# TensorE's order in the attention of a hybrid block: an even spread, and an order from a model of three engines' clocks

## The chip, the cores and the metric

One core of one Trainium2 chip runs the whole program. The metric is the device time of one execution in microseconds. The kernel before took 2173.42 us (median of 3 runs, 2172.76 to 2175.5). Engines are named as the profile names them: PE is TensorE (PEld its weight loads), DVE is VectorE, ACT is ScalarE, POOL is GpSimd, SP is SyncE, whose queue issues most DMAs.

## What is computed

One block of a hybrid model in float32, for 1024 tokens of width 1024: a norm, a projection to nine streams, a gated linear recurrence with 8 heads, a stick-breaking attention with 16 heads of width 64, output projections and a gated feed-forward. The change lies in the attention:

```python
def stick_breaking(q, k, v):
    scale = 1.0 / float(np.sqrt(SB_DH))
    outs = []
    for blk in range(s_len // SB_BLOCK):          # 8 rows of 128 queries
        q0 = blk * SB_BLOCK
        end = q0 + SB_BLOCK
        z = jnp.einsum('bhqd,bhkd->bhqk', q[:, :, q0:end], k[:, :, :end]) * scale
        mask = kpos[None, :] < qpos[:, None]
        log_keep = jnp.where(mask, jax.nn.log_sigmoid(-z), 0.0)
        log_w = jax.nn.log_sigmoid(z) + lax.cumsum(log_keep, axis=3, reverse=True) - log_keep
        a = jnp.where(mask, jnp.exp(log_w), 0.0)
        outs.append(jnp.einsum('bhqk,bhkd->bhqd', a, v[:, :, :end]))
```

q and k are normalised per head before it.

## The kernel before

The program has a recurrence stage, then the attention, then the output projections and the feed-forward. The attention works on 8 pairs of heads (`p`), each with two heads (`j`), and each head on 4 groups (`g`) of two query rows (`i`) of 128. Four kinds of work of a pair stand on TensorE:

- A **score** (`chunk`, L739 and L740) multiplies a query row with 1 to 4 blocks of 128 keys into a PSUM bank `pz`, of which there are two. ScalarE then makes two sigmoids of it (L749: `kp`, what is kept, and `a`), VectorE runs a scan backwards over `kp` (L752 or L755) and multiplies `a` by it (L757). Four tiles `a` exist. A row of more than four blocks is cut into two chunks (`KEY_CHUNKS`), so a pair has 24 scores.
- A **turn** (L782) transposes the up to four blocks of `a` that belong to two key blocks and two query rows into a bank `pt` (two banks). ScalarE copies the high half `th` (L784), VectorE subtracts for the low half `tl` (L785), three tiles of each.
- An **apply** (L798 and L799) multiplies `th` and `tl` with the values into the bank `po`, of which there is one. The last apply of a group is followed by a copy on ScalarE (L803), an addition on VectorE (L804) and a store. `reads` puts an apply two turns behind its own turn; a pair has 20 of each.
- **Fill** is other work that needs no attention result: the projections of the next pair's keys and queries, and of values or gates, in steps of three matmuls with 512 columns (0.65 units) or with 256 (0.33 units). Between its steps stand the norms of the next pair: the key sums (L275, L276), the query sums (L668, whose operands GpSimd makes in L646 and L647), the roots on VectorE (L679 to L691), and the normalising of the keys (L701 to L708), whose results SP's DMAs copy to the other head. `at_fill` gives the units of fill after which each of these comes.

TensorE's order is that of the calls in the program; nothing reorders it. The other engines' orders are made from the program by a scheduler, with the split of a turn at high priority. `at_pair` returns one list: it spreads the scores of a group evenly over the reads of the group before it, with constants. `weave` then spreads the fill over that list in proportion to costs written beside each step (`1.954 * max(nb, 2) * 0.054` for a score, 0.406 for a turn, 0.583 for an apply), after 2.854 units of fill ahead of the first score.

Of the kernel before, what the change touches and what calls it, by code (L numbers as in the profile page):

```python
# [35 lines left out]
def hybrid_block(ctx, tc, x, norm1_gain, w_in, lb_logits, hg_out_norm, sb_q_norm, sb_k_norm,  # L36
# [3 lines left out]
    x, out = x[0], out[0]  # L40
# [14 lines left out]
    def pbank(tag, bufs=2):  # L55
        return pp.tile([P, HS], F32, tag=tag, bufs=bufs, name=tag)
# [293 lines left out]
    def hg_q(h):  # L350
        return proj_t(in_block(h * P), copy_half(hd[h], "q"))
# [309 lines left out]
    def at_qn(p, half):  # L661
        def go():
            d = ad[p]
            sq = d.pop(("sq", half))
            pq = pbank("pz")
            for i in range(4):
                for j in range(3):
                    nc.tensor.matmul(pq[:, 2 * i:2 * i + 2], sq[:, j, i * P:(i + 1) * P], blk2, start=j == 0, stop=j == 2)  # L668
            nc.vector.tensor_copy(d["nv"][:, 16 + 8 * half:24 + 8 * half], pq[:, 0:8])
        return [(0.86, go)]  # L670
# [55 lines left out]
    def at_pair(p):  # L726
        d = ad[p]
        v, rq = d["v"], d["rq"]
        rows_of = {}

        def chunk(j, g, i, end, nb, first):
            def go():
                kk = d["kk"][j]
                qhi, qlo = d["qh"][j][i // 4], d["ql"][j][i // 4]
                qs = slice((i % 4) * P, (i % 4 + 1) * P)
                k0, w = (end - nb) * P, nb * P
                n = max(w, 256)
                ps = pbank("pz")
                nc.tensor.matmul(ps[:, :n], qhi[:, qs], kk[:, k0:k0 + n], start=True, stop=False)  # L739
                nc.tensor.matmul(ps[:, :n], qlo[:, qs], kk[:, k0:k0 + n], start=False, stop=True)  # L740
                if first:
                    d["kp"] = kps[0]
                    kps.append(kps.pop(0))
                at0 = (NT - 1 - i) * P + k0
                kp = d["kp"][:, at0:at0 + w + 1]
                a = at.tile([P, HS], F32, tag="a", bufs=4, name="a")
                col = 2 * i + j
                for n_, t in enumerate((kp, a)):
                    nc.scalar.activation(t[:, 0:w], ps[:, 0:w], AF.Sigmoid, scale=rq[:, n_, col:col + 1])  # L749
                rev = kp[:, 0:w][:, ::-1]  # L750
                if first:
                    nc.vector.tensor_tensor_scan(rev, rev, dsel[:, HS - w:][:, ::-1], initial=0.0,  # L752
                                                 op0=ALU.mult, op1=ALU.max)
# [3 lines left out]
                nc.vector.tensor_mul(a[:, 0:w], a[:, 0:w], kp[:, 1:w + 1])  # L757
# [12 lines left out]

        def turn(j, g, m):
            def go():
                tp = pbank("pt")
                th = at.tile([P, HS], F32R, tag="th", bufs=3, name="th")
                tl = at.tile([P, HS], F32R, tag="tl", bufs=3, name="tl")
                c0 = P if m == g else 0
                for s, (kb, i) in enumerate([(2 * m + 1, 2 * g), (2 * m + 1, 2 * g + 1),
                                             (2 * m, 2 * g), (2 * m, 2 * g + 1)]):
                    if m == g and s == 0:
                        continue  # L780
                    a, b = rows_of.pop((j, i, kb))
                    nc.tensor.transpose(tp[:, s * P:(s + 1) * P], a[:, b * P:(b + 1) * P], ident)  # L782
                with tc.high_priority():
                    nc.scalar.copy(th[:, c0:], tp[:, c0:])  # L784
                    nc.vector.tensor_sub(tl[:, c0:], tp[:, c0:], th[:, c0:].bitcast(F32))  # L785
                d["t", j, g, m] = th, tl
            return 0.406, go

        def apply(j, g, m):
            def go():  # L790
                if m == g:
                    d["po"] = pbank("po", 1)
                po = d["po"]
                th, tl = d.pop(("t", j, g, m))
                for u in (1, 0):
                    kb, c0 = 2 * m + 1 - u, P if m == g and u == 0 else 0
                    sl = slice(256 * u + c0, 256 * u + 256)
                    nc.tensor.matmul(po[:, c0:256], v[:, kb, j, :], th[:, sl], start=kb == 2 * g, stop=False)  # L798
                    nc.tensor.matmul(po[:, c0:256], v[:, kb, j, :], tl[:, sl], start=False,  # L799
                                     stop=m == 0 and u == 0)  # L800
# [18 lines left out]
        for n, jg in enumerate(groups):  # L819
            a = reads(*jg)  # L820
            b = scores(*groups[n + 1]) if n + 1 < len(groups) else []
            length = sum(c for c, _ in a)
            own += [(start + length * (i + 0.5) / len(a), 1, i, s) for i, s in enumerate(a)]
            own += [(max(0.5, start + length * 0.855 * (i + 0.4) / len(b) - 0.039), 0, i, s)
                    for i, s in enumerate(b)]
            start += length
        return [s for *_, s in sorted(own, key=lambda x: x[:3])]

    def at_fill(p, mid):
        k, q = at_k(p), at_q(p)  # L830
        m = [s for f in mid for s in f()]
        out, t = k[:14] + at_kn(p, 0) + k[14:], 0.0
        extra = [(3.9, at_kn(p, 1)), (8.49, at_qn(p, 0)), (13.7, at_qn(p, 1) + at_roots(p)), (17.6, at_norm(p))]
        for s in q + m:
            while extra and t >= extra[0][0]:
                out += extra.pop(0)[1]
            out.append(s)
            t += s[0]
        return out

    weave([], at_fill(0, [lambda: at_v(0)]))
    for p in range(NPAIR):
        own = at_pair(p)
# [275 lines left out]
    for f in range(2, NF):  # L1119
        n = [(f + 1, m) for m in (1, 2)] if f + 1 < NF else []  # L1120
# [223 lines left out]
```

## Time and profile before

| what | value |
|---|---|
| median of 3 runs | 2173.42 us |
| the profiled execution, its own time | 2172.1 us |
| its span (first to last instruction) | 2170.3 us |
| mean granted clock of TensorE | 0.986 |
| recurrence and first projections, up to the attention's fill | 0 to 533 us |
| fill ahead of pair 0 | 533 to 585 us |
| attention, first score to last apply | 585.4 to 1222.0 us |
| output projections and feed-forward | 1222 to 2170 us |

In the profile's rows a group of instructions has its line, its engine, its operation, the tile it writes and those that it reads, and its count; a number in square brackets is the idle time of the engine just before it, with what ended it. Rows of waits have the total, the number of waits and the longest. The length of the attention is the distance between starts of pairs, which repeat with small differences: an even pair has 64 wide steps of fill, an odd one 32 wide and 64 narrow, and the last pair 48 wide ones and no norms.

### The profile page before, as it was taken

The numbers are of one execution on the slowest core, as the hardware profiler recorded it, in microseconds if no ns is written. First come the engines' busy times: TensorE is split into PE (matmuls) and PEld (weight loads), VectorE is DVE, ScalarE is ACT, GpSimd is POOL, SyncE is SP. The second block draws the span as 40 slices with busy tenths as digits, with TensorE's granted clock in tenths as the row PEclk, the third lists the DMA queues.
The fourth block names the chain that finished last, engine by engine and source line by source line (L and its number), as shares of the span: only waits on it lengthen the run. The fifth ranks groups of instructions, "written<-read, shape, count | busy, mean of one in ns | idle before, by whom it ended". The sixth has DMA issues, their size and how long they took to land. (4 is left out here: it accounts for less than half of the span.)

```text
span 2170.3 us, 29182 instructions
## 1 busy us (share of the span) xinstructions
PE 2050.4 (94%) x10981; PEld 1734.7 (80%) x10981; DVE 1459.1 (67%) x2108; ACT 1040.9 (48%) x1791; POOL 735.1 (34%) x488
## 2 busy tenths in 40 slices
PE   7999999999899999998998989989799999999999
PEld 7889798988877877877877778767688888887787
DVE  6575848575387787787787698999733333337975
ACT  4453444443366565565565554536433333333443
POOL 4443434353221121131221042142655555545000
PEclk9999999999999999999999999999899999999999
DMA  4211111122322232222222535513222312255221
GB/s 153 80 49 59 59 59 59 42 71 84 95 77 72 77 80 70 76 76 74 76 75 76 182 114 199 182 29 110 83 64 78 102 60 81 68 175 204 88 95 51
DMA packets 190605, 195.59 MB, mean 90 GB/s; under 512 B 11960, under 2 KB 135280, under 8 KB 190464
## 3 DMA queue, kind: packets, MB, share of 16 engines
q1 hardware_dynamic: 189456, 192.02, 28.4%
q8 instruction: 86, 1.41, 0.3%
q10 hardware_dynamic: 1008, 1.70, 0.2%
q14 instruction: 55, 0.45, 0.1%
HBM read 138.77 MB, written 38.14 MB: 82 GB/s over the span
## 5 line engine op out<-in xcount | busy, mean ns | idle before, releaser
L121 POOL TENSOR_TENSOR wl<-wr,wh 128x1024 fp32r<-128x1024 f32 x72 | 183.2, 2548 | 596.6 <-ACT wh L120 456.2
L138 PE MATMUL pd<-hT,wh 128*128 128x512 f32 (+1 forms) x920 | 377.3, 410 | 0.0
L140 PE MATMUL pd<-hT,wl 128*128 128x512 f32 (+1 forms) x920 | 357.6, 389 | 0.0
L139 PE MATMUL pd<-hT,wh 128*128 128x512 f32 (+1 forms) x920 | 357.2, 388 | 0.1
L887 ACT CAST wh<-u 128x512 fp32r<-128x512 f32 (+1 forms) x280 | 183.9, 684 | 229.1 <-PE po L140 68.2
L888 DVE TENSOR_TENSOR wl<-u,wh 128x512 fp32r<-128x512 f32 (+1 forms) x196 | 171.7, 912 | 51.1 <-ACT wh L887 46.2
L139 PE MATMUL pd<-u,wh 128*128 128x512 f32 x496 | 194.2, 392 | 10.5 <-DVE u L888 10.5
L140 PEld LDWEIGHTS pd<-hT,wl 128*128 128x128 f32 x920 | 174.2, 189 | 36.9
L138 PE MATMUL pd<-u,wh 128*128 128x512 f32 x496 | 194.6, 392 | 1.3 <-ACT c L1192 0.7
L139 PEld LDWEIGHTS pd<-hT,wh 128*128 128x128 f32 x920 | 175.6, 191 | 20.4 <-DVE hT L188 0.4
L138 PEld LDWEIGHTS pd<-hT,wh 128*128 128x128 f32 x920 | 175.3, 191 | 20.5 <-ACT hT L187 0.2
L884 POOL TENSOR_TENSOR u<-u,u 128x1024 f32<-128x1024 f32 (+1 forms) x46 | 105.8, 2318 | 193.4 <-DVE u L995 52.5
L752 DVE TENSOR_TENSOR_SCAN kp<-kp,dsel 128x512 f32<-128x512 f32 (+3 forms) x128 | 136.5, 1066 | 33.6 <-ACT kp L749 32.9
L749 ACT ACTIVATE kp<-pz,rq 128x128 f32<-128x128 f32 (+2 forms) x192 | 112.6, 587 | 80.9 <-PE pz L740 80.4
L138 PE MATMUL pd<-wh,hT 128*128 128x256 f32 x512 | 151.0, 295 | 0.0
L139 PE MATMUL pd<-wl,hT 128*128 128x256 f32 x512 | 147.0, 287 | 0.0
L140 PE MATMUL pd<-wh,hT 128*128 128x256 f32 x512 | 147.0, 287 | 0.0
L140 PE MATMUL pd<-u,wh 128*128 128x512 f32 x352 | 137.5, 391 | 0.0
L782 PE MATMUL pt<-ident,a 128*128 128x128 f32 x576 | 94.2, 282 | 37.3 <-DVE a L757 25.2
L757 DVE TENSOR_TENSOR a<-a,kp 128x128 f32<-128x128 f32 (+2 forms) x192 | 116.9, 609 | 16.9 <-ACT a L749 0.6
L784 ACT CAST th<-pt 128x512 fp32r<-128x512 f32 (+1 forms) x160 | 86.5, 547 | 85.3 <-PE pt L782 84.6
L782 PEld LDWEIGHTS pt<-ident,a 128*128 128x128 f32 x576 | 68.1, 143 | 67.6 <-DVE a L757 26.1
(266 smaller groups left out, 5097.9 us busy)
## 6 DMA issues: line engine op xcount, KB each, us to landing
wr<-in_w_in SPq DMA_DIRECT2D x72, 512.0 KB
u<-in_w_ffn_in SPq DMA_DIRECT2D x24, 512.0 KB
wr<-in_w_ffn_in SPq DMA_DIRECT2D x20, 512.0 KB
u<-in_w_ffn_out SPq DMA_DIRECT2D x10, 1024.0 KB
d_act<-c SPq DMA_DIRECT2D x33, 256.0 KB
u<-d_act SPq DMA_DIRECT2D x8, 1024.0 KB
qh<-qh SPq DMA_DIRECT2D x48, 128.0 KB
ql<-ql SPq DMA_DIRECT2D x48, 128.0 KB
```

Of the source, the lines that this page charges most:

```text
L121: nc.gpsimd.tensor_sub(lo, raw, hi.bitcast(F32))
L138: nc.tensor.matmul(ps, lh, rh, start=start, stop=False, skip_group_check=adds)
L139: nc.tensor.matmul(ps, lh, rl, start=False, stop=False, skip_group_check=adds)
L140: nc.tensor.matmul(ps, ll, rh, start=False, stop=stop, skip_group_check=adds)
L749: nc.scalar.activation(t[:, 0:w], ps[:, 0:w], AF.Sigmoid, scale=rq[:, n_, col:col + 1])
L752: nc.vector.tensor_tensor_scan(rev, rev, dsel[:, HS - w:][:, ::-1], initial=0.0, op0=ALU.mult, op1=ALU.max)
L757: nc.vector.tensor_mul(a[:, 0:w], a[:, 0:w], kp[:, 1:w + 1])
L782: nc.tensor.transpose(tp[:, s * P:(s + 1) * P], a[:, b * P:(b + 1) * P], ident)
L784: nc.scalar.copy(th[:, c0:], tp[:, c0:])
L884: e.tensor_tensor(raw(to), raw(a), raw(b), op=op)
L887: nc.scalar.copy(hi, src)
L888: e.tensor_sub(lo, src, hi.bitcast(F32))
```

## The change

`at_pair` now returns two lists, the scores and the reads, each in its own order. A new function, `flow`, takes the place of `weave` for the pairs. It keeps a clock each for TensorE, ScalarE and VectorE (`now`, which goes on from pair to pair), adds a written duration to them for each step that it calls, and chooses the next step by them: the next turn or apply when the model has its operands and its bank ready at most 0.05 us ahead of TensorE's clock, else the next score when fewer than four tiles `a` are held and one of the two banks is free, else one step of fill, else it moves TensorE's clock. What is left of the fill follows when scores and reads are used up. There is no fill ahead of a pair's first score any more. `at_fill` puts the norms later: 10.4, 15.4 and 19.5 units in place of 8.49, 13.7 and 17.6. The steps themselves are unchanged, and so is the number of instructions on every engine.

```diff
@@ at_pair @@
-            return 1.954 * max(nb, 2) * 0.054, go
+            return go
...
-                    steps.append(chunk(j, g, i, end, nb, end == i + 1))
+                    steps.append(((j, i, end - nb, nb), chunk(j, g, i, end, nb, end == i + 1)))
...
-            return 0.406, go
+            needs = [(j, i, kb) for kb in (2 * m + 1, 2 * m) for i in (2 * g, 2 * g + 1) if kb <= i]
+            return "turn", (j, g, m), needs, go
...
-            return 0.583, go
+            return "apply", (j, g, m), [], go
...
-        own, start, at_time = [(0.0, 0, n, s) for n, s in enumerate(scores(*groups[0]))], 1.0, 1.0
...
-            own += [(start + length * (i + 0.5) / len(a), 1, i, s) for i, s in enumerate(a)]
-            own += [(max(0.5, start + length * 0.855 * (i + 0.4) / len(b) - 0.039), 0, i, s)
-                    for i, s in enumerate(b)]
-            start += length
-        return [s for *_, s in sorted(own, key=lambda x: x[:3])]
+        return [s for jg in groups for s in scores(*jg)], [s for jg in groups for s in reads(*jg)]
+    now = {"pe": 0.0, "act": 0.0, "dve": 0.0}
+    def on(e, ready, took):
+        now[e] = max(now[e], ready) + took
+        return now[e]
+    def flow(score, read, fill):
+        made, split_at, left = {}, {}, {}
+        pz, pt, po = [0.0, 0.0], [0.0, 0.0], [0.0]
+        while score or read:
+            ready = None
+            if read:
+                kind, at_, needs, go = read[0]
+                if kind == "turn":
+                    ready = max([made.get(b, 1e9) for b in needs] + [min(pt)])
+                else:
+                    ready = max([split_at[at_]] + (po if at_[2] == at_[1] else []))
+            if read and ready <= now["pe"] + 0.05:
+                read.pop(0)
+                go()
+                if kind == "turn":
+                    end = on("pe", 0.0, 0.109 * len(needs) + 0.1)
+                    w = 0.15 + 0.0012 * 90 * len(needs)
+                    end = on("dve", on("act", end, w), w + 0.08)
+                    split_at[at_] = end + 0.3
...
+                else:
+                    end = on("pe", 0.0, 0.48)
...
+            elif score and len(left) < 4 and min(pz) <= now["pe"] + 0.05:
+                c, go = score.pop(0)
+                go()
+                left[c] = c[3]
+                end = on("pe", 0.0, 0.114 * max(c[3], 2))
+                end = on("act", end, 2 * (0.26 + 0.109 * c[3]))
...
+                end = on("dve", end, 0.47 + 0.38 * c[3])
+                for b in range(c[2], c[2] + c[3]):
+                    made[c[0], c[1], b] = end + 0.4
+            elif fill:
+                c, go = fill.pop(0)
+                go()
+                t0 = now["pe"]
+                on("pe", 0.0, 1.05 * c)
+                on("act", t0, 0.3 * c)
+                on("dve", t0, 0.25 * c)
+            else:
...
+        for c, go in fill:
+            go()
...
-        extra = [(3.9, at_kn(p, 1)), (8.49, at_qn(p, 0)), (13.7, at_qn(p, 1) + at_roots(p)), (17.6, at_norm(p))]
+        extra = [(3.9, at_kn(p, 1)), (10.4, at_qn(p, 0)), (15.4, at_qn(p, 1) + at_roots(p)), (19.5, at_norm(p))]
...
-        weave(own, fill, lead=2.854)
+        flow(*at_pair(p), fill)
```

TensorE in pair 0, the first head's group 1, at its first turn. Before, a fill step, a three-block score and another fill step stand ahead of the three transposes (of `a`, into `pt`):

```order
L138 MATMUL pd<-hT_101,wh 128x512
L139 MATMUL pd<-hT_102,wh 128x512
L140 MATMUL pd<-hT_101,wl 128x512
L739 MATMUL pz<-kk,qh 128x384
L740 MATMUL pz<-kk,ql 128x384
L138 MATMUL pd<-hT_101,wh 128x512
L139 MATMUL pd<-hT_102,wh 128x512
L140 MATMUL pd<-hT_101,wl 128x512
L782 MATMUL pt<-ident,a 128x128 x3
```

Now the last of four fill steps and the apply of group 0 stand there, and two turns follow each other (an apply's lines are one higher in the changed kernel):

```order
L138 MATMUL pd<-hT_101,wh 128x512
L139 MATMUL pd<-hT_102,wh 128x512
L140 MATMUL pd<-hT_101,wl 128x512
L799 MATMUL po<-th,v 128x256
L800 MATMUL po<-tl,v 128x256
L799 MATMUL po<-th,v 128x128
L800 MATMUL po<-tl,v 128x128
L782 MATMUL pt<-ident,a 128x128 x7
```

Both group 1's turns and the scores ahead of them have moved together into clumps, with the fill steps between the clumps.

TensorE in the same head's group 2, from its second turn on. Before, each turn and score has a fill step behind it:

```order
L782 MATMUL pt<-ident,a 128x128 x4
L138 MATMUL pd<-hT_99,wh 128x512
L139 MATMUL pd<-hT_100,wh 128x512
L140 MATMUL pd<-hT_99,wl 128x512
L739 MATMUL pz<-kk,qh 128x384
L740 MATMUL pz<-kk,ql 128x384
```

Now two scores, the third turn and the group's first apply follow the second turn without fill, and one fill step stands ahead of the second apply:

```order
L739 MATMUL pz<-kk,qh 128x512
L740 MATMUL pz<-kk,ql 128x512
L739 MATMUL pz<-kk,qh 128x384
L740 MATMUL pz<-kk,ql 128x384
L782 MATMUL pt<-ident,a 128x128 x4
L799 MATMUL po<-th,v 128x256
L800 MATMUL po<-tl,v 128x256
L799 MATMUL po<-th,v 128x128
L800 MATMUL po<-tl,v 128x128
L138 MATMUL pd<-hT_99,wh 128x512
L139 MATMUL pd<-hT_100,wh 128x512
L140 MATMUL pd<-hT_99,wl 128x512
```

The fill has left the way from the second turn to its apply.

ScalarE at that place: the weight cast, the evacuation of the next pair's keys (`kr`, `sq`), a sigmoid, and then the copies `th` of the turns. Before:

```order
L120 CAST wh<-wr 128x1024
L618 ACTIVATE kr<-pd,cols 128x512
L620 ACTIVATE sq<-pd 128x512
L749 ACTIVATE kp_4506<-pz,rq 128x512
L784 CAST th<-pt 128x384
L784 CAST th<-pt 128x512
```

Now:

```order
L784 CAST th<-pt 128x384
L120 CAST wh<-wr 128x1024
L618 ACTIVATE kr<-pd,cols 128x512
L620 ACTIVATE sq<-pd 128x512
L749 ACTIVATE kp_4506<-pz,rq 128x512
L784 CAST th<-pt 128x512 x2
```

The first turn's copy has moved ahead of the key evacuation; the second turn's copy stands behind it and a sigmoid. At the end of each pair, on TensorE, 12 wide fill steps (26 narrow ones in an odd pair) now follow the last apply without anything between them, where one or two wide or narrow ones and then the 5 ahead of the next pair's first score stood.

More of the change, by code (lines that the diff above doesn't have):

```diff
@@ L817, in at_pair @@
         groups = [(j, g) for j in range(2) for g in range(4)]
-        own, start, at_time = [(0.0, 0, n, s) for n, s in enumerate(scores(*groups[0]))], 1.0, 1.0
[L819 to L822, printed above, removed]
-            own += [(start + length * (i + 0.5) / len(a), 1, i, s) for i, s in enumerate(a)]
-            own += [(max(0.5, start + length * 0.855 * (i + 0.4) / len(b) - 0.039), 0, i, s)
-                    for i, s in enumerate(b)]
-            start += length
@@ L827, in at_pair @@
-        return [s for *_, s in sorted(own, key=lambda x: x[:3])]
+        return [s for jg in groups for s in scores(*jg)], [s for jg in groups for s in reads(*jg)]
[4 more added lines that the diff above has]
+    def flow(score, read, fill):
+        score, read, fill = list(score), list(read), list(fill)
+        made, split_at, left = {}, {}, {}
[16 more added lines that the diff above has]
+                    split_at[at_] = end + 0.3
+                    pt.remove(min(pt))
+                    pt.append(end)
+                    for b in needs:
+                        c = next(c for c in left if c[0] == b[0] and c[1] == b[1] and c[2] <= b[2] < c[2] + c[3])
+                        left[c] -= 1
+                        if not left[c]:
+                            del left[c]
+                else:
+                    end = on("pe", 0.0, 0.48)
+                    if at_[2] == 0:
+                        end = on("act", end, 0.37)
+                        on("dve", end, 0.41)
+                        po[0] = end
+            elif score and len(left) < 4 and min(pz) <= now["pe"] + 0.05:
[4 more added lines that the diff above has]
+                end = on("act", end, 2 * (0.26 + 0.109 * c[3]))
+                pz.remove(min(pz))
+                pz.append(end)
+                end = on("dve", end, 0.47 + 0.38 * c[3])
[9 more added lines that the diff above has]
+            else:
+                now["pe"] = max(now["pe"], min([x for x in [ready, min(pz)] if x and x > now["pe"]], default=0.0)) + 0.01
+        for c, go in fill:
+            go()
+            t0 = now["pe"]
+            on("pe", 0.0, 1.05 * c)
+            on("act", t0, 0.3 * c)
+            on("dve", t0, 0.25 * c)
@@ L842, in hybrid_block @@
     for p in range(NPAIR):
-        own = at_pair(p)
         if p == NPAIR - 1:
```

## The prediction

> **What bounds the kernel now.** I read the page first for the length of the run and for the engine that fills it.
>
> ```profile
> span 2170.3 us, 29182 instructions
> PE 2050.4 (94%) x10981; PEld 1734.7 (80%) x10981; DVE 1459.1 (67%) x2108; ACT 1040.9 (48%) x1791; POOL 735.1 (34%) x488
> ```
>
> TensorE (PE) is said to be busy for 94% of 2170.3 us, so any gain must be idle time of TensorE. The edit touches only the attention, so next I cut the span by stage with the view of windows. The attention's first score stands at 585.4 and its last apply ends at 1222.0. The cuts inside are the starts of pairs: 667.23 (pair 1), 748.00 (pair 2), 830.33 (pair 3), 1157.64 (pair 7). A row has the stretch, its length, then busy time of PE, PEld, DVE, ACT and POOL, the granted clock, the DMA share and GB/s.
>
> ```profile
> 585.00:1220.00 635.00, 585.91 (x3549) 500.31 (x3548) 495.87 (x813) 396.36 (x767) 138.29 (x88) 0.98 0.28 75
> 667.23:748.00 80.77, 76.09 (x518) 68.50 (x516) 63.17 (x110) 50.94 (x100) 17.80 (x13) 0.98 0.25 64
> 748.00:820.00 72.00, 65.31 (x367) 53.53 (x366) 61.75 (x99) 47.15 (x92) 16.93 (x12) 0.98 0.31 82
> 748.00:830.33 82.33, 75.64 (x421) 62.34 (x420) 63.55 (x102) 50.32 (x96) 19.21 (x13) 0.98 0.32 87
> 1157.64:1222.00 64.36, 58.32 (x331) 48.03 (x330) 52.73 (x75) 42.14 (x83) 6.63 (x4) 1.00 0.17 53
> ```
>
> The reader is to see two things. TensorE idles 635.0 - 585.9 = 49.1 us in the attention, four tenths of the 119.9 us that it idles in the whole run. And inside pair 2 VectorE (DVE) is busy 61.75 of the first 72.00 us, but 63.55 - 61.75 = 1.80 of the last 10.33: while attention work lasts, VectorE runs at 86%. What TensorE waits for is in the view of waits, for this stage:
>
> ```profile
> PE pt L782 <- DVE a L757: 25.2, 27, 2.0
> PE pt L782 <- DVE tl L785: 11.4, 15, 1.5
> PE po L799 <- DVE tl L785: 5.0, 7, 1.0
> PE pz L668 <- POOL sq L647: 3.7, 3, 1.2
> PE pz L668 <- POOL sq L646: 2.3, 3, 0.8
> ```
>
> Turns wait for products of VectorE (25.2), turns wait for a free bank (11.4), applies wait for splits (5.0), and the query norm waits for GpSimd (6.0).
>
> Matmuls are pipelined, so a wait costs more than its idle time. I therefore rebuilt a pair from the distances between starts in stretches without waiting:
>
> ```profile
> 679.33 0.27 PE L798 MATMUL po<-th,v 128*128 128x256 f32 x1
> 679.73 0.44 PE L275 MATMUL pz<-sqh,blkr 128*128 128x512 f32 x1
> ...
> 681.29 0.27 PE L798 MATMUL po<-th,v 128*128 128x256 f32 x1
> ...
> 681.76 0.40 PE L138 MATMUL pd<-hT,wh 128*128 128x512 f32 x1
> ...
> 682.45 0.39 PE L739 MATMUL pz<-kk,qh 128*128 128x512 f32 x1
> ...
> 682.91 0.39 PE L138 MATMUL pd<-hT,wh 128*128 128x512 f32 x1
> ...
> 684.61 0.60 PE L782 MATMUL pt<-ident,a 128*128 128x128 f32 x4
> 684.97 0.48 PE L138 MATMUL pd<-hT,wh 128*128 128x512 f32 x1
> 685.28 0.39 PE L139 MATMUL pd<-hT,wh 128*128 128x512 f32 x1
> ...
> 685.75 0.33 PE L739 MATMUL pz<-kk,qh 128*128 128x384 f32 x1
> ...
> 686.10 0.39 PE L138 MATMUL pd<-hT,wh 128*128 128x512 f32 x1
> ...
> 742.29 0.28 PE L138 MATMUL pd<-wh,hT 128*128 128x256 f32 x1
> ...
> 742.65 0.28 PE L138 MATMUL pd<-wh,hT 128*128 128x256 f32 x1
> ```
>
> A wide fill step takes 682.45 - 681.76 = 0.69, a narrow one 0.36, a score of four blocks 0.46, of three 0.35 (so of two, and of one, which is padded to two, 0.23). A turn of four takes 684.97 - 684.61 = 0.36 and slows the matmul behind it from 0.23 to 0.31, so 0.44; a turn of three 0.33. An apply takes 0.47, the first of a group 0.40 (to 679.73); a key norm, two matmuls as wide as a fill step's, about 0.5. A pair has 24 scores (2 x (3 x 0.23 + 5 x 0.35 + 4 x 0.46) = 8.6), 20 turns (8 x 0.33 + 12 x 0.44 = 7.9), 20 applies (8 x 0.40 + 12 x 0.47 = 8.8) and two key norms (1.0): 26.3 us of its own; the narrow query matmuls, under 1 us, are left out. An even pair has 64 wide fill steps (44.2), an odd one 32 wide and 64 narrow (22.1 + 23.0), pair 7 in the old order 43 wide behind its first score (29.7) and no norm. Gapless this is 70.5, 71.4 and 55.0 us against 82.3, 80.8 and 64.4. **What TensorE loses is 11.8, 9.4 and 9.4 us a pair**, 4 x 11.8 + 3 x 9.4 + 9.4 = 85 us in all. That is the ceiling of this edit.
>
> **The change, part by part.** No instruction is added or removed; 192 scores, 160 turns, 160 applies and the fill steps stand in another order on TensorE, and the other engines' queues follow. Outside the attention only the fill ahead of pair 0 moves, by its norms.
>
> *Scores to turns.* In the order of before, group 1's first turn stands behind its last score (four blocks) by three wide steps, an apply and a score, 3 x 0.69 + 0.40 + 0.35 = 2.8 us, and waits there, in pair 1 for 1.13 us:
>
> ```profile
> 675.81 0.55 PE L782 MATMUL pt<-ident,a 128*128 128x128 f32 x3 [1.13 <-DVE a L757]
> ```
>
> In the new order there stand seven wide steps, a turn, two scores and an apply, 7 x 0.69 + 0.33 + 0.35 + 0.23 + 0.40 = 6.1 us. What VectorE has to do for a chunk, and the start of a pair, are these rows:
>
> ```profile
> L752 DVE TENSOR_TENSOR_SCAN kp<-kp,dsel 128x512 f32<-128x512 f32 x36 | 49.7, 1382 | 1.2 <-ACT kp L749 0.9
> L785 DVE TENSOR_TENSOR tl<-pt,th 128x512 fp32r<-128x512 f32 x72 | 49.2, 683 | 23.1 <-ACT th L784 22.8
> L752 DVE TENSOR_TENSOR_SCAN kp<-kp,dsel 128x384 f32<-128x384 f32 x36 | 40.0, 1111 | 5.9 <-ACT kp L749 5.8
> L757 DVE TENSOR_TENSOR a<-a,kp 128x512 f32<-128x512 f32 x48 | 37.4, 779 | 4.1 <-ACT a L749 0.6
> L757 DVE TENSOR_TENSOR a<-a,kp 128x384 f32<-128x384 f32 x60 | 34.4, 573 | 5.3 <-ACT th L784 0.5
> ```
>
> Four blocks are 1.38 + 0.78 = 2.16 us, three are 1.68. A four-block score with a three-block one queued ahead and a split makes some 4.5 us, plus its way through ScalarE: 6.1 covers it, 2.8 did not. So most of the 25.2 and 11.4 us should go.
>
> *Turns to applies.* The shortest way from a turn to its finished split, with both engines waiting for it, is this (822.28 to 823.53 + 0.69 = 1.94 us):
>
> ```profile
> 822.28 0.60 PE L782 MATMUL pt<-ident,a 128*128 128x128 f32 x4
> 822.91 0.59 ACT L784 CAST th<-pt 128x512 fp32r<-128x512 f32 x1 [2.34 <-PE pt L782]
> 823.53 0.69 DVE L785 TENSOR_TENSOR tl<-pt,th 128x512 fp32r<-128x512 f32 x1 [2.24 <-ACT th L784]
> ```
>
> Here the new order is not everywhere good. In group 2 the second turn is followed by two scores, a turn, an apply and one fill: 0.44 + 0.46 + 0.35 + 0.44 + 0.40 + 0.69 = 2.8 us to its apply, while ScalarE's queue has three operations about as long as the copy ahead of it, two of the key's evacuation and a sigmoid, some 2 us. 1.94 + 2 - 2.8 leaves 1.1; with VectorE late as well I take 1.7 us. In the second half of a pair the same place has even less cover (about 1 us), the last group's first turn finds a VectorE with three chunks, two splits and root steps to do (nothing to 1.5, I take 1), and the last applies have 1.75 us of cover against 1.94 (0.5). **Stalls left: 1.7 + 1 + 1 + 0.5 = 4.2 us a pair**; from below nothing, from above the 11.8 of now.
>
> *Fewer handovers.* Turns stand in 16 runs a pair in place of 20: 4 x 0.08 = 0.3 us.
>
> *Later query and key norms.* The first query norm moves from 8.49 to 10.4 units of fill; half 0 of the query then has 8 fill steps (5.5 us) and some 4 us of scores, turns and applies for GpSimd in place of 6 steps. The 6.0 us of waits are inside the 85 and are taken to go. The fill ahead of pair 0 has the same wait, in the view of waits from 533 to 586:
>
> ```profile
> PE pz L668 <- POOL sq L646: 2.1, 2, 1.7
> PE pz L668 <- POOL sq L647: 1.5, 2, 1.0
> ```
>
> Of these 3.6 us I take 2 to go: six more narrow steps, 2.2 us, stand ahead of the second query norm there. That is between nothing and 3.6.
>
> Key normalisation comes later on VectorE, behind the last four splits, and the next pair's first score needs its copies. 12 wide or 26 narrow fill steps (8.3 or 9.4 us) now stand after the last apply, and hide that.
>
> *What is late next: VectorE.* Those 12 steps have no attention work beside them. So pair 2 cannot be shorter than VectorE's work before them:
>
> ```profile
> 667.23 0.28 PE L739 MATMUL pz<-kk,qh 128*128 128x256 f32 x1
> ...
> 668.07 0.42 DVE L752 TENSOR_TENSOR_SCAN kp<-kp,dsel 128x128 f32<-128x128 f32 x1 [3.93 <-ACT kp L749]
> ```
>
> 0.84 to its first scan, 63.55 of work less 0.4 that falls behind the last apply, 0.6 to end that apply, 8.3 of fill: 72.9 us plus its idle time. Today it idles 72.0 - 61.75 - 0.84 = 9.4 us in that stretch. TensorE's way gives 70.5 - 0.3 + 4.2 = 74.4; VectorE's way with half its idle time gives 72.9 + 4.7 = 77.6. I take 76 for an even pair. For an odd one 71.4 - 0.3 + 4.2 = 75.3 and 0.84 + 63.17 - 0.4 + 0.6 + 9.4 + 4.7 = 78.3: I take 77. Pair 7 has 48 fill steps and none left at its end: 33.1 + 25.3 - 0.3 + 4.2 = 62.3 and the uncovered last applies, so 62.5.
>
> **Sum.** Now: 3.4 us of fill ahead of pair 0 and 4 x 82.3 + 3 x 80.8 + 64.4, 639.4 us. Then: 4 x 76 + 3 x 77 + 62.5 = 597.5. **42 us less, and 2 ahead of pair 0: 44.** The profiled execution took 2172.1 us, so 2128; the median of the runs is 2173.4, 1.3 above it, so 2129.
>
> **Rivals.**
>
> *VectorE idles as it does now.* It waits for ScalarE, which waits for TensorE, and clumps of two scores and two turns may only move that. Against it: VectorE's waits shown above (22.8 for the first halves of splits) come where turns were late. Price: 72.9 + 9.4 = 82.3, odd 83.0, pair 7 66: 644 against 639, so 2170 to 2178: no change within what can be measured (0.2%).
>
> *Clumps make handovers late: slower.* Place: the eight groups of a pair, at the first apply behind two turns and two scores. If the split comes 2 us later than the cover at each, a pair loses 16 us in place of 11.8 or 9.4 and is 70.5 - 0.3 + 16 = 86.2, 4 us more in an even pair and by the same sum 6 in the others: 41 in all, 2214. It decides from 1.2 to 1.5 us of lateness a group (8 x 1.2 = 9.6, 8 x 1.5 = 12, today's losses). For it speaks the 2 us of ScalarE's queue in group 2; against it that fill steps stand four together behind most clumps.
>
> *The granted clock.* Today each of pairs 1 to 6 has one dip, after idle time:
>
> ```profile
> 790.00:794.00 4.00, 2.02 (x21) 1.36 (x20) 3.79 (x6) 2.41 (x5) 1.87 (x2) 1.00 0.76 200
> 794.00:798.00 4.00, 4.00 (x16) 3.31 (x17) 3.33 (x10) 1.65 (x4) 0.00 (x0) 0.57 0.35 82
> ```
>
> TensorE is busy half of 790 to 794, and the clock is 0.57 in the next 4 us, which costs 0.43 x 4 = 1.7 us. If clumps of turns give two dips a pair in place of one, 1.7 x 8 = 14 us come back: 2143. The Trainium skill, TensorE: Matmul & The Clock Gate, section "HAM oscillation — how this bites in real kernels", says that an idle window throttles the array again, and its Part 4 on PE-mode transpose that transposes do not count as work there. By that rule seven transposes in a row speak against this change; the trace agrees as far as the dip follows half-idle microseconds, and no run here shows transposes alone doing it.
>
> **How the numbers follow.** The forecast case, from a quarter of the gain to the end of all of VectorE's idle time, 0.73, the clock's rival 0.09, no change 0.08, slower 0.10. Lower end: with no idle time left, pairs of 72.9 and 73.6 and 59.5 for pair 7 make 572, 67 us less, 2 more ahead of pair 0: 2104, and 2100 for VectorE work that shrinks beside GpSimd. Upper end: a quarter of the expected gain, 2163. Above it lie 0.18, below 0.02. Faster 0.82, same 0.08, slower 0.10.
>
> **What would show it.** The waits of turns for products and for splits fall from 36.6 to under 15 us in the attention, those of the query norm from 6.0 to under 1; the dips of the clock in the middle of pairs vanish; starts of pairs lie 75 to 78 us apart; what waits remain stand at the applies of the third group. VectorE over 90% busy up to the last apply would show that it is the bound; the same 86%, the first rival. The forecast is wrong if those waits only change their names, above all to applies waiting for splits.

## The result, and the profile after

| kernel | median, us | runs | ratio to before, 95% interval |
|---|---|---|---|
| before | 2173.75 | 4, from 2172.76 to 2175.5 | |
| changed | 2185.03 | 4, from 2184.41 to 2186.14 | 1.0052, 1.0034 to 1.0069 |

The changed kernel is slower by half a per cent, where 2% less was forecast. The page of its profiled execution begins:

```profile
span 2182.6 us, 29156 instructions
...
PE 2055.1 (94%) x10981; PEld 1743.8 (80%) x10981; DVE 1475.6 (68%) x2108; ACT 1032.3 (47%) x1791; POOL 731.5 (34%) x488
```

The span is 12.3 us longer and no share says why. The cut by stage does: the attention of before, from its first score to its last apply, in the view of windows (length, then busy time of PE, PEld, DVE, ACT and POOL, granted clock, DMA share, GB/s),

```profile
585.43:1222.00 636.57, 587.48 (x3559) 501.79 (x3558) 495.87 (x813) 396.73 (x767) 137.86 (x88) 0.98 0.28 74
```

and the attention of the changed kernel in the same view, with two of its pairs (2 and 4) and eight microseconds of pair 2:

```profile
579.81:1236.70 656.89, 599.38 (x3575) 517.36 (x3574) 508.78 (x815) 391.73 (x771) 139.02 (x89) 0.96 0.27 73
749.55:835.21 85.66, 77.48 (x422) 64.87 (x421) 65.34 (x104) 49.29 (x97) 19.84 (x13) 0.94 0.29 79
922.98:1005.22 82.24, 74.66 (x422) 62.70 (x421) 65.01 (x104) 49.30 (x97) 20.86 (x13) 0.98 0.31 83
774.00:778.00 4.00, 3.13 (x9) 2.65 (x10) 3.45 (x6) 1.23 (x3) 0.00 (x0) 0.50 0.29 84
778.00:782.00 4.00, 4.00 (x15) 3.21 (x14) 3.66 (x5) 1.19 (x3) 0.00 (x0) 0.67 0.00 0
```

The attention starts 5.6 us earlier (3.4 of it is the fill that stood ahead of pair 0 and now stands inside) and is 20.3 us longer; what follows it takes 945.9 us in place of 948.3. 20.3 - 5.6 - 2.4 = 12.3, the whole difference of the spans. Inside, TensorE idles 656.89 - 599.38 = 57.5 us where it idled 49.1, and is busy 11.9 us more, 3.4 of them for the fill that now stands inside and 8.5 for the same matmuls as before, at a clock of 0.96 in place of 0.98. Pairs 2 and 4 hold the same 422 matmuls: at 0.94 they take 77.5 us of busy time, at 0.98 74.7. The last two rows are one dip, at a third group's second apply, of which more below. By the trace's clock records the attention of before spends 20.4 us at half the clock, in 6 dips (stretches at half the clock), and that of the changed kernel 51.0 us, in 13 dips of 3.4 or 6.8 us. In each trace these dips start whole multiples of 3.41 us apart.

What TensorE waits for in the changed kernel's attention (engine, tile and line of the waiting instruction, what it waited for; total, number, longest):

```profile
PE po L800 <- DVE tl L785: 18.8, 7, 2.7
PE pz L739 <- DVE nv L669: 15.8, 11, 2.2
PE pz L668 <- ACT a L749: 7.1, 7, 1.1
PE pz L739 <- ACT a L749: 5.9, 6, 2.4
PE pt L782 <- DVE a L757: 5.4, 3, 1.8
PE pt L782 <- DVE tl L785: 1.7, 1, 1.7
PE po L799 <- ACT th L784: 1.6, 7, 0.2
```

The turns' waits are nearly gone, 36.6 us before and 7.1 now, in 4 waits where there were 42. In their place stand applies that wait for splits (18.8, one wait of 2.7 us in each pair with norms), and scores and query norms that wait for a bank `pz` (15.8 + 7.1 + 5.9 = 28.8). L669 is the copy that frees the bank of the query norm's sums, and L749 the second sigmoid, which frees a score's bank.

The place of the longest of these waits, that of the applies, in the timeline of the changed kernel's pair 2 (start, duration, engine, line, operation):

```profile
768.56 0.60 PE L782 MATMUL pt<-ident,a 128*128 128x128 f32 x4
...
769.53 0.68 ACT L618 ACTIVATE kr<-pd,cols 128x512 f32<-128x512 f32 x1
...
769.71 2.38 POOL L121 TENSOR_TENSOR wl<-wr,wh 128x1024 fp32r<-128x1024 f32 x1 [14.38 <-PE pz L740]
...
770.11 0.59 ACT L620 ACTIVATE sq<-pd 128x512 f32<-128x512 f32 x1
...
770.59 0.69 ACT L749 ACTIVATE kp<-pz,rq 128x512 f32<-128x512 f32 x1
770.73 1.64 DVE L270 CAST sqh<-sq 128x512 fp32r<-128x512 f32 x1 [2.12 <-ACT sq L620]
...
771.16 1.08 ACT L784 CAST th<-pt 128x512 fp32r<-128x512 f32 x2
...
772.41 0.69 DVE L271 TENSOR_TENSOR sql<-sq,sqh 128x512 fp32r<-128x512 f32 x1
...
773.02 1.22 DVE L752 TENSOR_TENSOR_SCAN kp<-kp,dsel 128x512 f32<-128x512 f32 x1
...
774.15 1.26 DVE L785 TENSOR_TENSOR tl<-pt,th 128x512 fp32r<-128x512 f32 x2
...
774.87 0.58 PE L800 MATMUL po<-tl,v 128*128 128x256 f32 x1 [2.69 <-DVE tl L785]
```

The turn is done at 769.2. Its copy `th` stands behind two operations of the key's evacuation and a sigmoid on ScalarE and starts at 771.16, not 0.03 us after the turn; its split, the first of the two at 774.15, stands behind the cast and the subtraction of the key's squares (1.64 + 0.69) and a scan (1.22) on VectorE and ends about 774.8. The way that takes 1.94 us when both engines wait took 6.2 us here. The cast itself is slow: it runs beside GpSimd's subtraction (769.71 to 772.09). Of the 14 such casts in this attention seven run beside one and take 1.64 us each, the other seven take 0.42. The runs without that subtraction, e7 and e8, show what this costs. TensorE then stands for 2.69 us, and the matmul behind it takes 0.58 us where 0.28 is usual.

### The profile page after: what moved, and what is told of

It is laid out like the page before. It is cut to its first block, busy times and chain, and to the rows that moved or that the text cites. A ratio compares the mean times of both kernels' runs of the same rounds, so it can differ in the third digit from the quotient of the medians.

```text
span 2182.6 us, 29156 instructions
## 1 busy us (share of the span) xinstructions
PE 2055.1 (94%) x10981; PEld 1743.8 (80%) x10981; DVE 1475.6 (68%) x2108; ACT 1032.3 (47%) x1791; POOL 731.5 (34%) x488
## 4 chain that ended last, share of the span: by engine, by line
PE 70%; DVE 20%; ACT 4%; issue 4%; DMA 1%; POOL 0%; DVEq 0%; ACTq 0%; SPq 0%; POOLq 0%
PE pd L138 15%; PE pd L139 15%; PE pd L140 15%; PE pt L139 2%; PE pt L140 2%; PE pt L138 2%; DVE kp L752 2%; DVE wl L947 2%; PE pt L782 2%; DVE u L947 2%; DVE u L943 2%; PE po L800 2%; PE po L138 1%; PE po L139 1%; PE po L140 1%
## 5 line engine op out<-in xcount | busy, mean ns | idle before, releaser
L121 POOL TENSOR_TENSOR wl<-wr,wh 128x1024 fp32r<-128x1024 f32 x72 | 182.5, 2537 | 570.4 <-ACT wh L120 469.2
L139 PEld LDWEIGHTS pd<-hT,wh 128*128 128x128 f32 x920 | 176.6, 192 | 27.5 <-DVE hT L188 0.4
L757 DVE TENSOR_TENSOR a<-a,kp 128x128 f32<-128x128 f32 (+2 forms) x192 | 122.9, 644 | 15.2 <-DVE kp L752 0.5
L785 DVE TENSOR_TENSOR tl<-pt,th 128x512 fp32r<-128x512 f32 (+1 forms) x160 | 98.1, 629 | 50.2 <-ACT th L784 49.9
L749 ACT ACTIVATE kp<-pz,rq 128x128 f32<-128x128 f32 (+2 forms) x192 | 113.5, 591 | 37.2 <-PE pz L740 33.4
L139 PEld LDWEIGHTS pd<-u,wh 128*128 128x128 f32 x496 | 93.5, 189 | 32.1 <-DVE u L947 12.8
L120 ACT CAST wh<-wr 128x1024 fp32r<-128x1024 f32 x72 | 75.7, 1051 | 89.8 <-PE pd L139 50.6
```

The costliest lines, as they stand in the source:

```text
L120: nc.scalar.copy(hi, raw)
L121: nc.gpsimd.tensor_sub(lo, raw, hi.bitcast(F32))
L139: nc.tensor.matmul(ps, lh, rl, start=False, stop=False, skip_group_check=adds)
```

## The experiments

Each kernel is timed beside the kernel before, on the same chip: four executions, ten of e3 and e4. The kernel before has a median of 2174.1 to 2174.4 us on each of the three chips used, so times are compared across them. "Halved" is the time that the attention of the profiled execution spends at half the clock. VectorE's, ScalarE's and TensorE's line numbers move a little between kernels.

### e1 and e2: the order and the norms apart

e1 is the changed kernel with the norms of before, e2 the kernel before with the changed kernel's norms:

```diff
# e1, against the changed kernel
-        extra = [(3.9, at_kn(p, 1)), (10.4, at_qn(p, 0)), (15.4, at_qn(p, 1) + at_roots(p)), (19.5, at_norm(p))]
+        extra = [(3.9, at_kn(p, 1)), (8.49, at_qn(p, 0)), (13.7, at_qn(p, 1) + at_roots(p)), (17.6, at_norm(p))]
# e2, against the kernel before
-        extra = [(3.9, at_kn(p, 1)), (8.49, at_qn(p, 0)), (13.7, at_qn(p, 1) + at_roots(p)), (17.6, at_norm(p))]
+        extra = [(3.9, at_kn(p, 1)), (10.4, at_qn(p, 0)), (15.4, at_qn(p, 1) + at_roots(p)), (19.5, at_norm(p))]
```

> The changed order with the norms at their old places (8.49, 13.7 and 17.6 units of fill). If the later norms cost the time (the query norms now stand ahead of a score that needs the same two banks pz), most of the 11 us come back: about 2175. If the order itself costs it, by long waits that halve the granted clock and by VectorE operations that GpSimd holds, nothing changes or the old waits for GpSimd's squares (6 us in the attention, 3 ahead of it) return: 2184 to 2194.

> The order of before with the norms at their new places. If the later norms are good by themselves, the waits of the query norm for GpSimd (6.0 us in the attention and 3.6 ahead of it) and one dip of the clock ahead of pair 0 go: 2165 to 2170. If they are what makes the changed kernel slower, it goes up: above 2178.

Measured: e1 2189.28 us (1.0061, 1.0046 to 1.0076), e2 2159.2 us (0.9931, 0.9915 to 0.9948). The two parts pull in opposite directions. In the old order the later norms gain 15 us; in the new order they gain 4 (2189.3 to 2185.0). The new order costs 15 us with the norms of before and 26 with the later ones. e2 lies below the 2165 to 2170 expected. In e2 TensorE waits like this:

```profile
PE pt L782 <- DVE tl L785: 18.8, 19, 2.1
PE pt L782 <- DVE a L757: 15.6, 19, 1.6
PE po L799 <- DVE tl L785: 3.5, 9, 0.5
```

The waits for GpSimd's operands (6.0 us) are gone without any new one for a bank, and the waits that are left, 37.9 us, come in 47 pieces of 0.8 us on average. Halved: 10.2 us. The changed kernel's 18.8 us at the applies come in 7 pieces.

### e3: the norms' sums in the fill's banks

```diff
-            d["pn", half] = sum_rows(lambda: pbank("pz"), blkr, sq, at, 3)
+            d["pn", half] = sum_rows(dbank, blkr, sq, at, 3)
...
-            pq = pbank("pz")
+            pq = dbank()
```

> The changed kernel with the key and query norms in a bank of pd in place of pz. The waits of scores for the query norm's copy (15.8 us), of scores for a sigmoid (5.9) and of the query norm for a sigmoid (7.1) go. If they stand on the path, with the clock's dips behind them, 29 us less is the most, I expect 10 to 20: 2165 to 2175. If VectorE's backlog is what counts, the wait moves to the next turn and the time stays within 4 us of 2185.

Measured: 2169.86 us (0.9977, 0.9964 to 0.9991), 15 less than the changed kernel. The waits for L669 and those of the query norm are gone; scores wait for a sigmoid as before (7.5 us, where 5.9 were expected to go); the waits at the applies stand as they were, and a new one, of an apply for the addition that frees `po`, has come:

```profile
PE po L800 <- DVE tl L785: 18.8, 7, 2.7
PE po L799 <- DVE t L805: 11.1, 7, 2.0
PE pz L739 <- ACT a L749: 7.5, 13, 2.5
PE pt L782 <- DVE a L757: 5.5, 3, 1.8
...
```

So in this order the shared bank is worth 15 us, but 11 us more than the old order in e2 remain without it: the banks alone are not the cause.

### e4 and e6: the waits filled with useless work

e4 puts 26 matmuls whose result nobody reads into each pair of the changed kernel, at three places where TensorE waits; e6 puts 11 at one place into e3, in the pairs with norms:

```diff
+    def idle_mm(n):
+        ps = dbank()
+        for i in range(n):
+            nc.tensor.matmul(ps, hT[0][0][:, 0, 0:P], hT[0][0][:, 1, :], start=i == 0, stop=i == n - 1)
...
+                if (kind, at_) == ("turn", (0, 0, 0)):      # e4 alone
+                    idle_mm(7)
+                if (kind, at_) == ("apply", (0, 2, 1)):     # e4 and e6
+                    idle_mm(11)
...
+                if c[:3] == (1, 5, 0):                      # e4 alone
+                    idle_mm(8)
```

> The changed kernel with 26 useless wide matmuls a pair (8 x 26 x 0.23 us = 48 us of TensorE time in all) put where it waits: 7 ahead of the first turn of a pair, 11 ahead of the third group's second apply, 8 ahead of the second chunk of row 5 of the second head. If the halved clock behind long waits costs 10 to 15 us, the dips fall from 13 to about 6 and the time falls by 5 to 12 us though work was added. If the clock does not matter, the waits are filled at no gain and the parts that do not fit cost: 2185 to 2200.

> The changed kernel with the norms in pd and 11 useless wide matmuls (2.5 us) ahead of the third group's second apply, in pairs 0 to 6 alone. They fill a wait that is there in any case. If the halved clock behind that wait is a cost of its own, the halved time falls from 24 to about 10 us and the time from 2170 by 4 to 7 us. If not, the time stays within 2 us or rises by what does not fit the wait.

Measured: e4 2180.23 us (1.0022, 1.0013 to 1.0032), with 26 x 8 x 0.23 = 48 us more work on TensorE still 4.8 us less than the changed kernel; halved 10.2 us in place of 51.0, in 3 dips where about 6 were expected. It loses again where nothing waits: pair 7 takes 70.4 us, not 64.3. e6 is the cleaner one: 2157.23 us (0.9924, 0.9909 to 0.9938). Its attention and that of e3, in the view of windows, e3 first:

```profile
580.16:1215.76 635.60, 588.25 (x3575) 507.38 (x3574) 506.90 (x815) 390.24 (x771) 140.26 (x89) 0.98 0.28 75
```

```profile
579.80:1207.40 627.60, 594.99 (x3652) 514.67 (x3651) 508.54 (x815) 389.73 (x771) 139.48 (x89) 1.00 0.28 76
```

77 matmuls more, and the attention is 8.0 us shorter. The clock goes from 0.98 to 1.00, halved time from 23.8 to 3.4 us; half of that difference, 10.2 us, is what a halved clock takes from a busy TensorE, which is the size of the gain. By the medians the gain is 12.6 us, against 4 to 7 expected, because e3's executions scatter (2164.5 to 2177.4 us, clocks of 0.982 to 0.987) and the profiled one, at 0.987, is among its shortest; e6's lie within 2 us. So a long wait can be paid twice, once as idle time and once in the clock behind it, and the second payment is real. It is not made every time: a dip starts in, or within 1.0 us behind, each of the seven 2.7 us waits of the changed kernel, but only three of the same seven in e3's trace.

### e7 and e8: GpSimd's subtraction taken away

The low half of the fill's weights is made by GpSimd (L121). Beside it some of VectorE's operations are slow. In the changed kernel's pair 2:

```profile
797.01 2.37 POOL L121 TENSOR_TENSOR wl<-wr,wh 128x1024 fp32r<-128x1024 f32 x1 [6.63 <-ACT wh L120]
...
797.23 2.56 DVE L757 TENSOR_TENSOR a<-a,kp 128x384 f32<-128x384 f32 x1
...
799.72 1.09 DVE L755 TENSOR_TENSOR_SCAN kp<-kp 128x256 f32<-128x256 f32 x1
...
800.73 0.13 DVE L669 COPY nv<-pz 128x8 f32<-128x8 f32 x1
...
800.92 0.54 PE L739 MATMUL pz<-kk,qh 128*128 128x384 f32 x1 [2.24 <-DVE nv L669]
```

A product whose mean was 573 ns before takes 2.56 us and ends 0.4 us after the subtraction; a scan and the copy that frees the norm's bank stand behind it, and the next score waits 2.24 us. e7 (the changed kernel) and e8 (e2) leave the subtraction out and write zeros, in the attention and the fill ahead of it:

```diff
-        nc.gpsimd.tensor_sub(lo, raw, hi.bitcast(F32))
+        if last.get("att"):
+            nc.gpsimd.memset(lo.bitcast(F32), 0.0)
+        else:
+            nc.gpsimd.tensor_sub(lo, raw, hi.bitcast(F32))
```

> The changed kernel without the subtraction for the low half of the weights in the attention's stage on GpSimd (a memset of the low half stands in its place). If GpSimd holds VectorE's operations, most of the 51 us by which VectorE's operations are longer beside GpSimd go, and the part of it that is on the path: 10 to 25 us less than the changed kernel's 2185, 2160 to 2175. If not, the time stays at 2183 to 2187.

> The same in the old order with the norms at their new places (2159). If the new order loses because it puts more of GpSimd's subtractions beside VectorE's work (51 us of longer operations against 38), it gains less here than in the changed order: 5 to 12 us, 2147 to 2154, and the two orders come closer than the 26 us between them now. If the difference of the orders does not come from there, both gain alike and the 26 us stay.

Measured: e7 2142.56 us (0.9857, 0.9841 to 0.9874), 42 less than the changed kernel; e8 2128.67 us (0.9788, 0.9773 to 0.9802), 30.5 less than e2. Both gains are far above what was expected, 10 to 25 and 5 to 12. In e7's attention TensorE idles 27.5 us less than in the changed kernel's and is busy 16.9 less; halved time falls from 51.0 to 17.1 us. Of e7's waits these two are the ones that were 18.8 and 15.8 us (its lines are 3 higher):

```profile
PE po L803 <- DVE tl L788: 10.3, 7, 1.5
...
PE pz L742 <- DVE nv L672: 2.7, 5, 0.8
```

So in this order 8.5 us of the applies' wait and 13.1 of the scores' wait for the copy come of the subtraction. The groups of VectorE's operations that show it, with count, busy time, mean ns of one and idle time before them, in the attention of the kernel before,

```profile
L757 DVE TENSOR_TENSOR a<-a,kp 128x256 f32<-128x256 f32 x32 | 13.6, 426 | 2.8
L270 DVE CAST sqh<-sq 128x512 fp32r<-128x512 f32 x14 | 13.6, 974 | 12.3 <-ACT sq L620 12.3
...
L755 DVE TENSOR_TENSOR_SCAN kp<-kp 128x256 f32<-128x256 f32 x16 | 12.0, 750 | 2.0 <-ACT kp L749 1.2
```

of the changed kernel,

```profile
L755 DVE TENSOR_TENSOR_SCAN kp<-kp 128x256 f32<-128x256 f32 x16 | 27.0, 1690 | 0.0
...
L757 DVE TENSOR_TENSOR a<-a,kp 128x256 f32<-128x256 f32 x32 | 20.6, 644 | 2.6
...
L270 DVE CAST sqh<-sq 128x512 fp32r<-128x512 f32 x14 | 14.4, 1031 | 14.9 <-ACT sq L620 14.9
```

and of e7:

```profile
L760 DVE TENSOR_TENSOR a<-a,kp 128x256 f32<-128x256 f32 x32 | 15.2, 476 | 2.6
L758 DVE TENSOR_TENSOR_SCAN kp<-kp 128x256 f32<-128x256 f32 x16 | 12.3, 767 | 0.0
...
L273 DVE CAST sqh<-sq 128x512 fp32r<-128x512 f32 x14 | 5.9, 424 | 14.6 <-ACT sq L623 14.6
```

The same scan takes 1690 ns in the changed order and 767 without the subtraction, so it is the subtraction that holds it: seven of the 16 run beside one and take 2.85 us, eight beside no work of GpSimd and take 0.75. In the old order none of the 16 runs beside one (750). Without the subtraction the two orders are 13.9 us apart (2142.6 and 2128.7) where they were 25.8: the hold makes 12 of the 26 us. The old order was expected to lose little by it; it loses 30 us. The Trainium skill, SBUF — State Buffer, section "Who interferes with whom", has the rule: a VectorE operation with two inputs in SBUF contends with a GpSimd operation that reads SBUF, not with one that only writes it; copies and casts in a two-port mode contend too, and whichever issues first keeps the shared ports for its whole instruction. These runs agree for the operations with two inputs: the product takes 2.56 us beside a subtraction that reads two tiles, and in e7 six products of the same size beside a memset take 0.56 us, as they do alone. For the cast they agree in the first half, 1.64 us beside a subtraction and 0.42 without; no cast of e7 ran beside a memset. What GpSimd does for the query norm (L646 and L647) holds VectorE as well and stays in e7, e8 and e10: six products of 128x384 beside its squares take 1.28 us in e7.

### e5, e9 and e10: a model that charges what the fill does when it does it

`flow` adds 0.3 us of ScalarE and 0.25 us of VectorE to the clocks for each unit of fill. The real work comes in bursts when a projection is complete: two operations of 0.6 to 0.7 us on ScalarE and two on VectorE for a key half, as the timeline above shows, and ahead of them only a weight cast of 1.05 us on ScalarE. e9 gives the steps that carry such work its duration, read from the traces, and charges it there; e5 does the same with the norms in the fill's banks, as in e3:

```diff
-                on("act", t0, 0.3 * c)
-                on("dve", t0, 0.25 * c)
+                a, v = getattr(go, "cost", (0.0, 0.0))
+                on("dve", on("act", now["pe"], a) if a else 0.0, v)
...
+        steps[0][1].cost = (1.05 if half == 0 else 0.0, 0.0)      # weight cast
...
+        evac.cost = (1.2, 1.7)      # key half; a query half (1.2, 0.75), values (0.75, 0.85), gates (0.6, 0)
...
+        go.cost = (0.6, 0.0)        # key norm; a query norm (0, 0.2), roots (0, 2.6), normalising (1.3, 3.4)
```

> The changed kernel with the norms in pd, and with a model that charges the fill's evacuations, weight casts, roots and normalisations to ScalarE and VectorE where they fall, in place of 0.3 and 0.25 a unit everywhere. If the wait of 2.7 us at the third group's second apply (18.8 us in all with the norms in pd) comes from the key's evacuation that the model smears, it falls under 5 us, dips of the clock fall with it, and the time goes from 2170 to 2150 to 2160, level with the old order with new norms. If the order in clumps is bad by itself, the time stays at 2165 to 2175.

> The changed kernel with the fill's bursts charged in the model, but the norms in the banks pz as in the changed kernel. If the banks are a cost of their own (15 us between 2185 and 2170), the time is 2155 to 2165, some 15 us above the 2145 with both. If the model's better times for VectorE have moved scores away from the query norms, the banks cost less than 5 us more: 2145 to 2150.

Measured: e5 2145.12 us (0.9866, 0.9852 to 0.9881), below the 2150 to 2160 expected, e9 2143.07 us (0.9859, 0.9844 to 0.9874). e9 is 42 us below the changed kernel, 31 below the one before and 16 below e2: the fastest kernel of this study with the whole computation in it. Its attention takes 613.1 us, halved 6.8. Its waits (its lines from `at_pair` on are 11 higher than the changed kernel's, so L811 is the apply that was L800, L793 the turn):

```profile
PE pt L793 <- DVE a L768: 7.9, 10, 1.2
PE pt L793 <- DVE tl L796: 6.8, 10, 1.2
PE po L810 <- DVE t L816: 5.7, 4, 1.5
PE pz L750 <- ACT a L760: 3.4, 5, 2.4
PE pt L793 <- DVE nv L690: 2.5, 3, 0.9
PE pz L676 <- ACT a L760: 2.4, 4, 0.6
PE po L811 <- DVE tl L796: 1.0, 3, 0.4
...
```

The applies' wait for splits has gone from 18.8 us to 1.0 and the scores' wait for the norm's copy is no longer in the list, though the norms are in the scores' banks as they were. So in this order the banks are no cost of their own: the 15.8 us were another consequence of steps that the model thought early and VectorE had late, most of it by the hold (2.7 us are left of them in e7). e9 still has the hold, so the order alone keeps it off these two places. e9 is even a little below the 2145 to 2150 expected of that case. That it isn't slower than e5 lies within the intervals.

e10 is e5 without GpSimd's subtraction in the attention, the edit of e7:

> The order with bursts and norms in pd, without GpSimd's subtraction for the weights' low half in the attention. If GpSimd's hold on VectorE costs every order 30 to 40 us, 2105 to 2118; if this order has its fill where VectorE idles, so that the hold costs it less, 2120 to 2135.

Measured: 2114.78 us (0.9726, 0.9709 to 0.9742), 30 less than e5, as the first of the two cases expected. The hold is worth as much in the mended order as in the old one (30.5), and 12 us less than in the changed order. Order and hold are two matters that met in the changed kernel: the first is mended in e9, the second costs 30 us in the orders of e2 and e5 too.

## Why the prediction was wrong

**The ceiling** of 85 us was rightly counted, and it can be set beside the outcome. With 3.4 us of fill, before took 640.0 us as measured (639.4 by the prediction's typical pairs) against 554.6 without gaps (4 x 70.5 + 3 x 71.4 + 58.4 for a last pair with 48 steps). Half of the halved time is an estimate of what the clock took; the changed kernel and e7 bear it out, with 33.9 us of halved time and 16.9 us of busy time between them.

| us | before | changed | forecast |
|---|---|---|---|
| over the gapless time | 85.4 | 102.3 | 42.9 |
| TensorE idle | 49.1 | 57.5 | |
| half of the halved time | 10.2 | 25.5 | |
| rest (matmuls slowed at handovers and behind waits, not split further) | 26.1 | 19.3 | |

**Scores to turns** held: 36.6 us were to fall under 15 and fell to 7.1. **Later query norms** held as far as they went: no wait for GpSimd is left in the attention, and the start ahead of pair 0 gained 5.6 - 3.4 = 2.2 us where 2 were taken. e2 shows the whole edit worth 15 us in the old order.

**The step that failed is the sum of TensorE's stalls under "Turns to applies", 4.2 us a pair, and under it the model that I took over without weighing it.** TensorE's waits in the list above are 56.3 us, 7.0 a pair, and the clock takes another 25.5, 3.2 a pair, for which the sum had nothing: it had the dips of before vanish. The forecast's own sign of being wrong came true, waits that change their names to applies waiting for splits. The sum had the right place (the third group's second apply) with 1.7 us for it; it waits 2.7 (18.8 / 7). I summed ScalarE's queue there (two of the key's evacuation and a sigmoid, some 2 us), but for VectorE only rounded 1.1 up to 1.7, where the same evacuation puts 1.64 + 0.69 us and a scan, 3.55 us, ahead of the split. Of the 1.64, 1.2 is GpSimd's hold on the cast, which I put at nothing; without it, in e7, the apply waits 1.5 us (10.3 / 7), inside the 1.7. The rows of the diff showed why no order from this model could know: the fill's work is smeared evenly over its steps. I read these two lines, and costed three places by hand, as if the rest were planned by true clocks. e9 changes those charges and nothing else, and 42 us go, with the hold still there. With them the change reaches 31 of the 44 us that I expected of it; with the charges that it has, it gives all of that back and 11 more.

**Banks** were missed altogether. The prediction moved the norms past scores and never asked which bank holds their sums; 15.8 us of scores' waits for L669, 7.1 of query norms' and 5.9 of scores' for L749 stand there, 28.8 of the 56.3. Of the 15.8, 13.1 need the hold as well (e7).

**"VectorE is late next"** took 76 and 77 us a pair. Pairs took 82.2 to 87.8, and VectorE's busy share stayed near its old value: 508.78 / 656.89 is 77%, 495.87 / 636.57 was 78%. What was not in the sum was that VectorE's work itself would grow, by 12.9 us: without the subtraction VectorE is busy 41.8 us less in e7 and 28.3 less in e8, and the difference, 13.5, is about this growth. The lower end of the range named work beside GpSimd, but only as something that might shrink.

**The rivals.** "Clumps make handovers late" was the right direction with the wrong place: not at all eight groups by 2 us, but at one apply by 2.7 and at bank waits. "The granted clock" came true in size, 15 us by half of 51.0 - 20.4, but not from clumps of turns as I wrote it, nor from transposes: e6 gets the clock back by filling one wait, with every turn where it was. The Trainium skill, TensorE: Matmul & The Clock Gate, section "HAM oscillation — how this bites in real kernels", asks for no idle gap over about 3.4 us. Here the waits were shorter, 2.7 us at the longest, and in the changed kernel each of these seven had a halved stretch of 3.4 or 6.8 us at its end all the same; the measurement decides. In e3 four of the same seven had none. Many waits of 0.8 us, as in e2, left 10.2 us halved; what pattern of shorter gaps just suffices, and whether it depends on where the gap falls among the multiples of 3.41 us, was not tried.

**Left open:** how the 26 us between the orders divide beyond GpSimd's 12 (clock and idle time overlap, and filling a wait changes both); and whether a kernel with e9's order that frees VectorE of the hold while still computing the low halves keeps the 30 us of e10. That was not tried.

## What to carry to other kernels

An order made by a model is as good as the bursts in it: charge each operation of the other engines where it is issued, above all the evacuations behind a projection, and then look in the trace for the one place that every round of the loop waits at. When a step is moved, list what it holds as well as what it waits for (a bank, a queue place, a port), since others wait for that. And count a wait of two or three microseconds with the slower clock that may follow it, so that the same idle time in many short pieces is likely the cheaper one.

## What the runs showed of the hardware

Useless work can pay: 77 matmuls put into waits made e6's attention 8.0 us shorter, by 20.4 us less at half the clock. A wait of 2.24 us of TensorE can begin two engines away: a 2.37 us subtraction on GpSimd stretched a product on VectorE to 2.56 us, where 0.55 is usual, and leaving out the 32 such subtractions of the attention, with those in the fill ahead of it, took 30 to 42 us off the kernel.
